# A gated Fourier and Hyena encoder layer: where ScalarE's sigmoids and operand roundings stand in the F and H projections

## The chip, the cores and the metric

The kernel runs on one core of one Trainium2 chip. The metric is the device time of one execution, in microseconds, lower is better. A core has five engines with a queue each, and a queue is worked through in order: TensorE (PE in the profile, its weight loads PEld), VectorE (DVE), ScalarE (ACT), GpSimd (POOL) and SyncE (SP). Here SP and POOL issue the transfers (DMA) of the stage in question.

## The reference, cut to what matters

Two sequences of 1024 rows of 1024 channels (`x_prompt` and `x_sample`) go through the same layer. Only its end bears on this change:

```python
def encoder_layer(x, ...):
    p = rmsnorm(x, g_pre) @ w_in
    fv, fg, hv, hg, mg = jnp.split(p, ...)
    ...                                       # fz: 2-D Fourier transform of fv; z: Hyena branch of hv
    y_f = (fz * jax.nn.silu(fg)) @ w_fourier_out
    y_h = (z * jax.nn.silu(hg)) @ w_hyena_out
    g_f, g_h = jnp.split(jax.nn.sigmoid(mg + b_merge), 2, axis=-1)
    out = (g_f * y_f + g_h * y_h) @ w_out
    return x + rmsnorm(out, g_post)
```

All arrays are float32.

## The kernel before, in words

The phases run one after the other: the Fourier transform, the Hyena branch with its filters, the gates of the second sequence (`phase_gates`), and `phase_out`, which holds the two projections `y_f` and `y_h` and then, in `last_rows`, the product with `w_out`, the norm and the residual. The gates' raw values (`mg` before bias and sigmoid) and the operands `fz * silu(fg)` and `z * silu(hg)` lie in DRAM tensors `d_g` and `d_sh` by then.

A float32 product is made of three matmuls of rounded numbers. `split` (line 168) rounds a tile on ScalarE (line 171, a CAST in the trace) to its high part and subtracts that on VectorE (line 181) to get the low part; `mm3` then multiplies high by high, high by low and low by high.

`phase_out` goes over four units: two sequences, two halves of 512 positions each. Each unit has two passes of eight tiles. The F pass (`pyf`, operands `sf`, weights `w_fo`) makes the eight 128-channel tiles of `y_f`, the H pass (`pyh`, operands `sh`, weights `w_ho`) those of `y_h`. That is 64 tiles in all. In a tile, `project` (line 1115 on) asks `weight` for two halves of the weights (128 x 512 each: a DMA on POOL's queue at line 1108, rounding on ScalarE, subtraction on VectorE), and each half feeds 12 matmuls, so a tile has 24. There are three buffers for weight halves: two in the pool `wp`, one in `op`, taken in turn by the counter `nw`.

Around the matmuls of a tile stand:

- `operand` (line 1090 on): loads one of the eight operand tiles that the *next* pass will read (DMA on SP's queue, line 1097) and rounds it at once. Operands have one buffer each for F and for H, so a load can go once the last pass that read the buffer is over.
- `gated` (line 1123): loads the gate tile `g` (line 1126, SP's queue, three buffers), takes its sigmoid in place on ScalarE (line 1127), and multiplies with the sums on VectorE.
- in the H pass, an add of the two products into `yf` and its store to `d_m` (line 1209, SP's queue).
- `beside` (line 1136): in units 1 and 2, preparation of `w_out` for the last stage, four blocks in all: a load `oraw` at tile 1 or 9 and, two tiles later, casts `bh` and `th` on ScalarE and sums and subtractions (`osum`, `bl`, `tl`) on VectorE; in unit 3 similar work for `t1` and, in `sum4`, for `t4`. Its ScalarE instructions are kept behind the tile's sigmoid, its loads behind the gate's load.

The order of instructions in each engine's queue is not simply that of the program. A planner orders all of them by program order as priority and by its own estimate of times. `tc.issue_after(x)` adds only this: the instructions in its block that run on x's engine come later in that engine's queue than x. Instructions of the block on other engines are not bound by it.

Of the kernel before, what the change touches and what calls it, by code (L numbers as in the profile page):

```python
# [9 lines left out]
F32 = mybir.dt.float32  # L10
F32R = mybir.dt.float32r
I32 = mybir.dt.int32
AF = mybir.ActivationFunctionType
# [148 lines left out]
class K:  # L162
# [626 lines left out]
    def conv_back(self, n, ct, B, ws):  # L789
# [3 lines left out]
        for g, pairs in GROUPS:  # L793
# [34 lines left out]
            def tt(name):  # L828
                return ws.tile([P, 512], F32, tag="tt", name=name, bufs=4)
# [3 lines left out]
            elif g == 3:  # L833
                S_, D_ = tt("S"), T[1]
                self.add("dve", S_, T[1], Tp)
# [243 lines left out]
    def phase_out(self):  # L1079

        tc, nc, a = self.tc, self.nc, self.a
        wp, xp = self.wp, self.xp
        units = [(b, half) for b in range(NB) for half in range(2)]
        with ExitStack() as es:
            pool = lambda n: es.enter_context(tc.tile_pool(name=n, bufs=1, reuse_waits="tile"))
            bl, sp, oc, sc, op = pool("bl"), pool("sp"), pool("oc"), pool("sc"), pool("op")
            self.nw = 0

            def operand(i, nm, k):

                b, half = units[i]
                src = (self.d_g[b][0] if nm == "f" else self.d_g[b][4] if b else self.d_sh[b])[k][:, 512 * half:512 * half + 512]
                t = xp.tile([P, 2, 512], F32R, tag=f"x{'hl'[k // 4]}{k % 4 + 4 * (nm == 'h')}", name=f"s{nm}{k}", bufs=1)
                r = t[:, 1].bitcast(F32)
                nc.sync.dma_start(r, src)
                self.split(t[:, 0], t[:, 1], r, "dve", "act")
                return t[:, 0], t[:, 1]

            def weight(w, dt, q):


                own = self.nw % 3 == 2
                self.nw += 1
                pool, nb = (op, 1) if own else (wp, 2)
                r = pool.tile([P, 512], F32, tag="w", name="wr", bufs=nb)
                nc.gpsimd.dma_start(r, a[w][dt][:, 512 * q:512 * q + 512])
                h = pool.tile([P, 4, P], F32R, tag="wh", name="wh", bufs=nb)
                l = pool.tile([P, 4, P], F32R, tag="wl", name="wl", bufs=nb)  # L1110
                self.split(h.rearrange("p a b -> p (a b)"), l.rearrange("p a b -> p (a b)"), r, "dve", "act")
                return h, l

            def project(i, nm, w, dt, S):
                ps = self.psum("mm", 4, f"py{nm}")
                for q in range(2):
                    h, l = weight(w, dt, q)
                    for kk in range(4):
                        k = 4 * q + kk
                        self.mm3(ps, (h[:, kk], l[:, kk]), S[k], k == 0, k == 7)  # L1120
                return ps

            def gated(i, dt, ps, sec, bias, out):
                b, half = units[i]
                g = wp.tile([P, 512], F32, tag="gt", name="g", bufs=3)
                self.fetched = nc.sync.dma_start(g, self.d_g[b][sec][dt][:, 512 * half:512 * half + 512])
                self.opened = nc.scalar.activation(g, g, AF.Sigmoid, bias=self.bm[:, bias:bias + 1])
                out = g if out is None else out
                self.mul("dve", out, ps, g)
                return out  # L1130

            BH, BL, TH, TL = [], [], [], []

            def beside(i, dt):

                with tc.issue_after(self.fetched.ins), tc.issue_after(self.opened.ins):
                    if i in (1, 2):
                        k, part = 2 * i - 2 + dt // 8, dt % 8  # L1140
                        if part == 1:
                            self.raw = load(k)
                        elif part == 3:
                            blocks(k, self.raw)
                    if (i, dt) == (3, 1):
                        T1.append(sum1())
                    elif (i, dt) == (3, 4):
                        h, l = T1.pop()
                        for k in range(4):
                            self.split(h[:, k], l[:, k], l[:, k].bitcast(F32), "dve", "act")  # L1150
                            T1.append((h[:, k], l[:, k]))

            def load(k):
                r = sc.tile([P, 4, 512], F32, tag="raw", name="oraw", bufs=1)
                for i in range(2):
                    nc.sync.dma_start(r[:, 2 * i:2 * i + 2].rearrange("p a b -> p (a b)"),
                                      a["w_out"][(k + 4 * i) * P:(k + 4 * i + 1) * P])
                return r

            def blocks(k, r):  # L1160
                s = sc.tile([P, 4, 512], F32, tag="sum", name="osum", bufs=1)
                h, l = [bl.tile([P, 3, 512], F32R, tag=f"{t}{k}", name=f"{t}{k}", bufs=1) for t in ("bh", "bl")]
                self.split(h[:, 0], l[:, 0], r[:, 0], "dve", "act")
                self.split(h[:, 1:3], l[:, 1:3], r[:, 2:4], "dve", "act")
                BH.append(h)
                BL.append(l)
                self.sums(s, r)
                h, l = [bl.tile([P, 2, 512], F32R, tag=f"{t}{k}", name=f"{t}{k}", bufs=1) for t in ("th", "tl")]
                self.split(h, l, s[:, 1:3], "dve", "act")
                TH.append(h)  # L1170
                TL.append(l)
                for j in range(2):
                    nc.sync.dma_start(self.d_t[j][:, k], s[:, 3 * j])

            T1, T4 = [], []

            def sum1():
                h, l = [sc.tile([P, 4, 512], F32R, tag=t, name=n, bufs=1) for t, n in (("raw", "t1h"), ("sum", "t1l"))]
                nc.sync.dma_start(l.bitcast(F32), self.d_t[0])
                return h, l  # L1180

            def sum4(k):
                h, l = [sp.tile([P, 512], F32R, tag=f"yf{2 * k + j}", name=f"t4{'hl'[j]}{k}", bufs=1) for j in range(2)]
                r = l.bitcast(F32)
                nc.sync.dma_start(r, self.d_t[1][:, k])
                self.split(h, l, r, "dve", "act")
                T4.append((h, l))

            with tc.issue_after(self.copied.ins):
                S = {(0, "f"): [operand(0, "f", k) for k in range(8)]}  # L1190
            gp = oc.tile([P, D], F32, name="gp")
            nc.sync.dma_start(gp, a["g_post"][0].partition_broadcast(P))
            for i, (b, half) in enumerate(units):
                Yf = []
                S[i, "h"] = []
                for dt in range(8):
                    ps = project(i, "f", "w_fo", dt, S[i, "f"])
                    S[i, "h"].append(operand(i, "h", dt))
                    y = sp.tile([P, 512], F32, tag=f"yf{dt}", name=f"yf{dt}", bufs=1)
                    Yf.append(gated(i, dt, ps, 5, dt, y))  # L1200
                    beside(i, dt)
                S[i + 1, "f"] = []
                for dt in range(8):
                    ps = project(i, "h", "w_ho", dt, S[i, "h"])
                    if i + 1 < len(units):
                        S[i + 1, "f"].append(operand(i + 1, "f", dt))
                    g = gated(i, dt, ps, 6, 8 + dt, None)
                    self.add("dve", Yf[dt], Yf[dt], g)
                    nc.sync.dma_start(self.d_m[i][:, :, dt], Yf[dt].rearrange("p (t c) -> p t c", t=4))
                    beside(i, 8 + dt)  # L1210
                    if i == 3 and dt % 2 == 1:
                        sum4(dt // 2)
            block = lambda j: [(BH[k][:, j], BL[k][:, j]) for k in range(4)]
            T = [[(TH[k][:, j], TL[k][:, j]) for k in range(4)] for j in range(2)]
            self.last_rows(units, block(0), block(1), block(2), T1, T[0], T[1], T4, gp, op)
# [196 lines left out]
```

## Time and profile before

| | us |
|---|---|
| median of three runs | 2494.66 |
| lowest and highest of them | 2486.66, 2496.76 |
| the profiled execution, its own time | 2485.07 |
| span in its profile, first to last instruction | 2483.2 |
| granted TensorE clock | 0.997 of full |
| first and last matmul start of the two projections | 1955.5, 2319.5 |

The profile is of one execution. A row of its timeline reads: start in us, duration in us, engine, line of the kernel, operation, out<-in by the program's names, shapes, number of merged instructions, and in brackets how long the engine stood idle before it and what ended that. Rows of groups give the total busy time, the mean of one in ns, and the idle time just before. Tile names used here: `wr` raw weights, `wh` and `wl` their high and low parts, `g` a gate, `sf` and `sh` the operands, `oraw` raw `w_out`.

### The profile page before, as it was taken

What the parts mean: (1) busy time and instruction counts of PE and PEld (TensorE: products, weight loads), DVE (VectorE), ACT (ScalarE), POOL (GpSimd) and SP (SyncE); (2) the same over time, 40 slices, a digit from 0 to 9 for tenths busy, and PEclk for the clock granted to TensorE, in tenths of its full rate; (3) what the DMA queues carried; (4) which work ended last, traced back from release to release, by engine and by line L of the source; (5) the groups of instructions that cost most, each with busy time, mean ns of one, the idle gap of its engine ahead of it and who ended that gap; (6) DMA issues with size and microseconds to landing.
All of it is one profiled execution on the core that took longest, in us unless ns stands there. A gap on an engine that the chain in (4) does not pass through costs nothing.

```text
span 2483.2 us, 37239 instructions
## 1 busy us (share of the span) xinstructions
PE 2407.4 (97%) x13184; PEld 2081.4 (84%) x13184; DVE 1955.9 (79%) x3737; ACT 1102.2 (44%) x2043; POOL 498.6 (20%) x514
## 2 busy tenths in 40 slices
PE   6999999999989999999999999999999999999998
PEld 6988888888878888888888888887888787878786
DVE  7786788888798999999889999876655456655677
ACT  5546666666653333333222233333443445444443
POOL 1331222212233333441000000212000111212121
PEclk9999999999999999999999999999999999999999
DMA  7536545444555554545343443435443567675543
GB/s 272 191 113 225 196 157 162 162 163 158 177 184 184 180 174 167 171 154 193 123 149 137 137 141 123 140 132 182 168 163 136 196 219 252 237 245 201 161 166 127
DMA packets 224867, 429.39 MB, mean 173 GB/s; under 512 B 23510, under 2 KB 87223, under 8 KB 224168
## 3 DMA queue, kind: packets, MB, share of 16 engines
q1 hardware_dynamic: 197868, 332.29, 40.1%
q0 software_dynamic: 26624, 94.70, 10.9%
q8 instruction: 104, 1.70, 0.3%
q14 instruction: 83, 0.68, 0.1%
q10 hardware_dynamic: 188, 0.02, 0.0%
HBM read 290.60 MB, written 136.31 MB: 172 GB/s over the span
## 4 chain that ended last, share of the span: by engine, by line
PE 44%; DMA 5%; DVE 3%; issue 1%; ACT 1%; SPq 0%; DVEq 0%; POOL 0%; ACTq 0%
PE pin L194 14%; PE pg L194 8%; PE po L194 6%; PE pyf L194 5%; PE pT L194 4%; PE pyh L194 4%; PE pX L194 3%; DMA oraw<-in_w_out 1%; PE tph L785 1%; DMA xraw<-d_x 1%; DMA mraw<-d_m 1%; DMA sh<-d_g 1%; DMA wr<-in_w_fo 1%; DMA wh<-d_w 0%; DMA d_m<-yf 0%
## 5 line engine op out<-in xcount | busy, mean ns | idle before, releaser
L194 PE MATMUL pin<-xh,wh 128*128 128x512 f32 x1440 | 563.8, 392 | 4.4 <-DVE v L177 1.8
L194 PE MATMUL pin<-xh,wl 128*128 128x512 f32 x1440 | 563.0, 392 | 1.6 <-POOL wl L181 1.6
L194 PE MATMUL pin<-xl,wh 128*128 128x512 f32 x1440 | 564.2, 392 | 0.0
L181 POOL TENSOR_TENSOR wl<-wr,wh 128x512 fp32r<-128x512 f32 x132 | 250.0, 1895 | 1132.2 <-ACT wh L171 1093.5
L194 PEld LDWEIGHTS pin<-xh,wh 128*128 128x128 f32 x1440 | 271.1, 188 | 54.6 <-DVE v L177 2.0
L194 PEld LDWEIGHTS pin<-xh,wl 128*128 128x128 f32 x1440 | 271.3, 188 | 51.6 <-POOL wl L181 2.5
L194 PEld LDWEIGHTS pin<-xl,wh 128*128 128x128 f32 x1440 | 271.3, 188 | 49.5
L171 ACT CAST wh<-wr 128x512 fp32r<-128x512 f32 x260 | 159.8, 618 | 227.2 <-PE pin L194 102.6
L194 PE MATMUL pT<-cinv,yh 128*128 128x256 f32 x1024 | 193.2, 283 | 0.5 <-ACT yh L171 0.5
L194 PEld LDWEIGHTS pT<-cinv,yh 128*128 128x128 f32 x1024 | 165.5, 191 | 10.1 <-ACT yh L171 0.9
L181 DVE TENSOR_TENSOR t<-pX,k 128x1024 f32<-128x1024 f32 x128 | 155.6, 1216 | 11.0 <-PE pX L194 7.6
L194 PE MATMUL pyh<-sh,wh 128*128 128x512 f32 x512 | 157.9, 391 | 3.5 <-ACT wh L171 3.5
L194 PE MATMUL pX<-bh,cfwd 128*128 128x256 f32 x768 | 160.4, 287 | 0.6 <-DVE t L181 0.6
L194 PE MATMUL pyf<-sf,wh 128*128 128x512 f32 x512 | 157.6, 391 | 1.6 <-ACT wh L171 1.6
L194 PE MATMUL pT<-cinv,yl 128*128 128x256 f32 x512 | 145.8, 285 | 5.1 <-DVE yl L181 5.0
L171 ACT CAST yh<-y 128x512 fp32r<-128x512 f32 x128 | 79.7, 622 | 158.6 <-DVE y L181 125.5
L171 ACT CAST bh<-b 128x512 fp32r<-128x512 f32 x144 | 88.9, 621 | 119.5 <-DVE b L181 81.2
L181 DVE TENSOR_TENSOR wl<-wr,wh 128x512 fp32r<-128x512 f32 x128 | 87.2, 686 | 67.1 <-ACT wh L171 67.0
L194 PEld LDWEIGHTS pX<-bh,cfwd 128*128 128x128 f32 x768 | 125.5, 190 | 4.0 <-DVE t L181 1.0
L181 DVE TENSOR_TENSOR bl<-b,bh 128x512 fp32r<-128x512 f32 x144 | 110.3, 767 | 21.9 <-ACT bh L171 21.8
L194 PEld LDWEIGHTS pyh<-sh,wh 128*128 128x128 f32 x512 | 95.5, 188 | 25.4 <-ACT wh L171 6.2
L194 PEld LDWEIGHTS pyf<-sf,wh 128*128 128x128 f32 x512 | 95.6, 188 | 23.1 <-ACT wh L171 3.7
(348 smaller groups left out, 5385.6 us busy)
## 6 DMA issues: line engine op xcount, KB each, us to landing
k<-d_k SPq DMA_DIRECT2D x128, 512.0 KB, 4.0
wr<-in_w_in SPq DMA_DIRECT2D x132, 256.0 KB, 3.1
d_g<-gt SPq DMA_DIRECT2D x124, 256.0 KB, 2.3
d_k<-kt SPq DMA_DIRECT2D x128, 128.0 KB, 2.2
d_k<-kt SPq DMA_DIRECT2D x64, 256.0 KB, 2.3
wr<-in_w_fo POOLq DMA_DIRECT2D x64, 256.0 KB, 3.6
g<-d_g SPq DMA_DIRECT2D x64, 256.0 KB, 3.9
wr<-in_w_ho POOLq DMA_DIRECT2D x64, 256.0 KB, 3.5
```

The source lines that it names most:

```text
L171: self.rounded = nc.scalar.copy(h, src)
L181: e.tensor_tensor(out, a, b, op=op)
L194: return self.nc.tensor.matmul(out, lhsT, rhs, start=start, stop=stop, skip_group_check=shared)
L785: nc.tensor.transpose(tp[:, q * P:(q + 1) * P], eo[:, e, q], self.ident)
```

## The change

Three things. First, `operand` only loads; its rounding is a function of its own, `rounded`. Second, a new function `ahead` is called once a tile: it rounds the operand that was loaded one tile earlier, with its ScalarE instruction placed behind the tile's second weight rounding (`self.weighed`), and then loads the next operand; after the pass one more call rounds the eighth. Third, the gate's sigmoid in `gated` is placed behind the same weight rounding. The first pass's eight operands are still rounded together.

```diff
                 t = xp.tile([P, 2, 512], F32R, ...)
-                r = t[:, 1].bitcast(F32)
-                nc.sync.dma_start(r, src)
-                self.split(t[:, 0], t[:, 1], r, "dve", "act")
+                nc.sync.dma_start(t[:, 1].bitcast(F32), src)
+                return t
+
+            def rounded(t):
+                self.split(t[:, 0], t[:, 1], t[:, 1].bitcast(F32), "dve", "act")
                 return t[:, 0], t[:, 1]
...
                 self.split(h..., l..., r, "dve", "act")
+                self.weighed = self.rounded
                 return h, l
...
+            def ahead(i, nm, dt):
+                S_ = S.setdefault((i, nm), [])
+                with tc.issue_after(self.weighed.ins):
+                    if dt:
+                        S_[-1] = rounded(S_[-1])
+                if dt < 8:
+                    S_.append(operand(i, nm, dt))
+
             def gated(i, dt, ps, sec, bias, out):
                 b, half = units[i]
                 g = wp.tile([P, 512], F32, tag="gt", name="g", bufs=3)
                 self.fetched = nc.sync.dma_start(g, ...)
-                self.opened = nc.scalar.activation(g, g, AF.Sigmoid, bias=...)
+                with tc.issue_after(self.weighed.ins):
+                    self.opened = nc.scalar.activation(g, g, AF.Sigmoid, bias=...)
...
-                S = {(0, "f"): [operand(0, "f", k) for k in range(8)]}
+                S = {(0, "f"): [rounded(operand(0, "f", k)) for k in range(8)]}
...
                 for dt in range(8):
                     ps = project(i, "f", "w_fo", dt, S[i, "f"])
-                    S[i, "h"].append(operand(i, "h", dt))
+                    ahead(i, "h", dt)
                     ...
+                ahead(i, "h", 8)
                 for dt in range(8):
                     ps = project(i, "h", "w_ho", dt, S[i, "h"])
                     if i + 1 < len(units):
-                        S[i + 1, "f"].append(operand(i + 1, "f", dt))
+                        ahead(i + 1, "f", dt)
                     ...
+                if i + 1 < len(units):
+                    ahead(i + 1, "f", 8)
```

More of the change, by code (lines that the diff above doesn't have):

```diff
@@ L1126, in gated @@
                 self.fetched = nc.sync.dma_start(g, self.d_g[b][sec][dt][:, 512 * half:512 * half + 512])
-                self.opened = nc.scalar.activation(g, g, AF.Sigmoid, bias=self.bm[:, bias:bias + 1])
+                with tc.issue_after(self.weighed.ins):
+                    self.opened = nc.scalar.activation(g, g, AF.Sigmoid, bias=self.bm[:, bias:bias + 1])
                 out = g if out is None else out
@@ L1194, in phase_out @@
                 Yf = []
-                S[i, "h"] = []
                 for dt in range(8):
                     ps = project(i, "f", "w_fo", dt, S[i, "f"])
-                    S[i, "h"].append(operand(i, "h", dt))
+                    ahead(i, "h", dt)
                     y = sp.tile([P, 512], F32, tag=f"yf{dt}", name=f"yf{dt}", bufs=1)
@@ L1201, in phase_out @@
                     beside(i, dt)
-                S[i + 1, "f"] = []
+                ahead(i, "h", 8)
                 for dt in range(8):
```

## The prediction

> **What bounds the kernel now.** The page comes first: TensorE (PE) is busy for 97% of the span, so time is won only where PE waits. The change touches one stage, the F and H projections, from 1955.4 to 2319.8 us.
>
> ```profile
> span 2483.2 us, 37239 instructions
> PE 2407.4 (97%) x13184; PEld 2081.4 (84%) x13184; DVE 1955.9 (79%) x3737; ACT 1102.2 (44%) x2043; POOL 498.6 (20%) x514
> ```
>
> Next, busy time by stretches: the whole stage first, then 25 us windows. The first pair after the times is PE busy and, in brackets, its matmuls; a window without a stall has 112.
>
> ```profile
> 1955.40:2319.80 364.40, 355.35 (x1539) 286.22 (x1538) 206.75 (x315) 167.91 (x270) 68.16 (x127) 1.00 0.68 227
> 1955.00:1975.00 20.00, 18.21 (x74) 13.10 (x74) 11.62 (x18) 12.70 (x20) 3.22 (x6) 1.00 0.81 294
> 1975.00:2000.00 25.00, 25.00 (x112) 20.71 (x111) 9.26 (x15) 8.68 (x14) 5.37 (x10) 1.00 0.46 149
> 2050.00:2075.00 25.00, 24.61 (x107) 19.56 (x106) 17.97 (x27) 14.29 (x24) 5.37 (x10) 1.00 0.76 258
> 2100.00:2125.00 25.00, 23.52 (x101) 18.28 (x101) 17.61 (x27) 12.60 (x20) 5.07 (x10) 1.00 0.68 213
> 2175.00:2200.00 25.00, 23.91 (x105) 19.30 (x104) 15.41 (x24) 10.91 (x19) 3.77 (x7) 1.00 0.75 261
> 2200.00:2225.00 25.00, 22.68 (x98) 17.97 (x98) 15.38 (x23) 11.45 (x18) 4.83 (x9) 1.00 0.66 209
> 2225.00:2250.00 25.00, 24.27 (x104) 18.95 (x104) 15.06 (x24) 14.46 (x25) 4.29 (x8) 1.00 0.80 277
> 2275.00:2300.00 25.00, 24.23 (x106) 19.45 (x105) 12.14 (x20) 8.76 (x14) 4.30 (x8) 1.00 0.69 221
> 2300.00:2325.00 25.00, 24.61 (x107) 19.69 (x107) 15.22 (x25) 8.90 (x15) 3.72 (x7) 1.00 0.58 183
> ```
>
> At 25/112 = 0.223 us a matmul, the missing ones cost: start (89.6 - 74) 3.5 us; near 2060 1.1; near 2110 2.5; near 2190 1.6 and 2202 3.1; near 2245 1.8; the end 1.3 + 1.1. Sum 16.0 us. All windows left out are full or lack one matmul. A second count comes from ScalarE's queue in undisturbed running:
>
> ```profile
> 2077.12 0.62 ACT L171 CAST wh<-wr 128x512 fp32r<-128x512 f32 x1 [2.05 <-PE pyf L194]
> 2078.18 0.73 ACT L1127 ACTIVATE g<-g,bm 128x512 f32<-128x512 f32 x1 [0.43 <-DMA g<-d_g]
> ...
> 2082.56 0.62 ACT L171 CAST wh<-wr 128x512 fp32r<-128x512 f32 x1 [2.05 <-PE pyf L194]
> ```
>
> Between these rows lies one more weight cast, left out; two casts make a tile: 2082.56 - 2077.12 = 5.44 us, 2.72 a half, 0.2267 a matmul. 1539 of them are 348.9 us, so 364.4 - 348.9 = 15.5 us are lost. About 16 us, 0.64% of the time, is therefore all that this stage has to give, unless the tile itself got shorter, and nothing in the change shortens it. The rows also show the order: a weight half is cast when PE has finished the half three before it (three buffers), and the sigmoid g sits between two such casts. By counting casts, the sigmoid of tile n stands behind the second cast of tile n-1 and ahead of both of tile n.
>
> Then the waits of the stage (1955 to 2322): who waited for whom, total, times, longest.
>
> ```profile
> ACT g L1127 <- DMA g<-d_g: 70.2, 49, 5.5
> ACT wh L171 <- PE pyf L194: 44.0, 32, 2.1
> ACT wh L171 <- PE pyh L194: 21.1, 15, 2.1
> ACT sh L171 <- DMA sh<-d_g: 14.0, 11, 3.9
> ACT sf L171 <- DMA sf<-d_g: 13.2, 11, 3.0
> ACT sh L171 <- DMA sh<-d_sh: 10.7, 9, 3.5
> ACT t4h L171 <- DMA t4l<-d_t: 8.2, 3, 3.7
> DVE osum L181 <- DMA oraw<-in_w_out: 3.7, 3, 1.9
> ```
>
> ScalarE stands 70.2 us at sigmoids and 14.0 + 13.2 + 10.7 = 37.9 us at operand casts, for loads. Mostly that is free, since weights run ahead. It is not free where several such waits meet the casts of an `oraw` block:
>
> ```profile
> 2107.16 0.73 ACT L1127 ACTIVATE g<-g,bm 128x512 f32<-128x512 f32 x1 [2.44 <-DMA g<-d_g]
> 2107.79 1.56 ACT L171 CAST bh<-oraw 128x512 fp32r<-128x512 f32 x2
> 2109.25 1.04 ACT L171 CAST th<-osum 128x1024 fp32r<-128x1024 f32 x1
> 2110.20 0.61 ACT L171 CAST wh<-wr 128x512 fp32r<-128x512 f32 x1
> 2110.86 0.73 PE L194 MATMUL pyh<-sh,wh 128*128 128x512 f32 x2 [0.82 <-ACT wh L171]
> 2199.09 0.73 ACT L1127 ACTIVATE g<-g,bm 128x512 f32<-128x512 f32 x1 [4.86 <-DMA g<-d_g]
> 2202.79 1.26 PE L194 MATMUL pyh<-sh,wh 128*128 128x512 f32 x4 [1.45 <-ACT wh L171]
> ```
>
> The weight cast at 2110.20 waited for nothing but its queue: a sigmoid held up by its load stood ahead of it, then 2.6 us of casts; PE started on that weight at 2110.86. The same happened at 2199 to 2202.
>
> **The change, part by part.** Durations:
>
> ```profile
> L181 DVE TENSOR_TENSOR wl<-wr,wh 128x512 fp32r<-128x512 f32 x127 | 86.5, 686 | 66.7 <-ACT wh L171 66.6
> L171 ACT CAST wh<-wr 128x512 fp32r<-128x512 f32 x127 | 77.5, 618 | 75.7 <-PE pyf L194 44.0 <-PE pyh L194 21.1 <-DMA wr<-in_w_ho 7.0
> L1127 ACT ACTIVATE g<-g,bm 128x512 f32<-128x512 f32 x64 | 46.5, 726 | 72.5 <-DMA g<-d_g 70.2 <-DVE wl L181 1.6 <-DVE g L181 0.3
> L171 ACT CAST sh<-sh 128x512 fp32r<-128x512 f32 x31 | 18.9, 623 | 24.9 <-DMA sh<-d_g 14.0 <-DMA sh<-d_sh 10.7
> ```
>
> Nothing is added or removed: the same 64 sigmoids (0.73 us), 56 operand casts (0.62) with their VectorE subtractions (0.69, as those of the weights), and all loads. Loads carry no new edge; they may leave when their buffers are free, as now. Only ScalarE's order gets lower bounds.
>
> *Sigmoids.* Tile n's moves behind the tile's own second weight cast, two casts or 5.44 us later. The longest wait of 5.5 us at the old place becomes about 0.1 if loads keep their times. Queued behind it then are an `oraw` block's casts (2.6 us) and the next tile's first weight, which becomes castable 2.72 us later and is needed 5.44 us after that; the chain behind a second weight is operand 0.62 + sigmoid 0.73 + block 2.6 = 3.95 us, so it is late by some 1.9 us at the four blocks and has 5.44 - 0.62 - 0.69 = 4.1 us in hand. The product that reads the sigmoid comes at the tile's end, 8 us after the new place: covered. Cost 0 on PE; if the loads were 5 us later still, the cover would be gone.
>
> *Operand casts.* Now all eight of a pass come when their buffers fall free, at the start of the pass before, in a bunch:
>
> ```profile
> 2053.55 1.23 DVE L181 TENSOR_TENSOR osum<-oraw 128x1024 f32<-128x1024 f32 x1 [1.91 <-DMA oraw<-in_w_out]
> 2057.82 2.49 DVE L181 TENSOR_TENSOR sh<-sh 128x512 fp32r<-128x512 f32 x4
> ```
>
> VectorE first stood for `oraw`, then did four operand subtractions in a row (2.49 us), which a weight's subtraction has to sit out. After the change one comes per tile, behind that tile's weights, so at most 0.69 us of operand work meets a weight. The wait for `oraw` stays. The last operand stands behind the pass's last weight, cast 3 halves (8.2 us) before PE reaches its next pass: covered.
>
> *The sum, against the 16.0 us.* Near 2060: 1.1 becomes 0.4 (`oraw` stays late). Near 2110: 2.5 becomes 0.3. Near 2190 and 2202: 4.7 becomes 0.8. Near 2245, a bunch of operand casts: 1.8 becomes 0.3. The end is not touched, since `t4h` gets no edge: its 2.4 us stay.
>
> ```profile
> 1962.98 1.29 ACT L171 CAST sh<-sh 128x512 fp32r<-128x512 f32 x2 [1.95 <-DMA sh<-d_sh]
> 1964.81 1.28 ACT L1127 ACT_TABLE_LOAD   x1
> 1966.10 0.72 ACT L1127 ACTIVATE g<-g,bm 128x512 f32<-128x512 f32 x1
> ```
>
> At the start the operand waits ahead of the weights go, but the first sigmoid needs only the first tile's weights ahead of it, so its load and the 1.28 us table load may now stand before the next weight; between 0 and 3.5 left, I take 2.0, nearer the rows' 1.28 + 0.72. Gains 0.7 + 2.2 + 3.9 + 1.5 + 1.5 = 9.8 us, less 0.3 for the late weight at the blocks: 9.5. The trace cannot show the new order's own waits: between -4 (every stall goes but the end's) and +5 us (0.1 a tile on 50 tiles), taken at 0.
>
> [...]
>
> The profiled execution took 2485.07 us (span 2483.2), 9.6 under the median of the three runs, 2494.66, which spread over 10 us. 2485.07 - 9.5 = 2475.6 in a like execution; from the median, **2485.2 us**.
>
> **The rivals.**
>
> *All of it goes.* With smoother VectorE the adds that free gate buffers come earlier, so loads and `t4h` too, and even the end tightens. For: bunches like the one at 2057.82 hold up VectorE's products and adds as well, on which SP's stores and the gate loads behind them wait. Against: the `oraw` and `t4h` waits have no edge in this change. Gain 15: 2479.7.
>
> *The gaps stay.* Three weight buffers, not the order, limit how far weights run ahead. For: ScalarE waited 44.0 + 21.1 us for PE to free them. Against: the casts just ahead of the stalls show no such wait (2110.20). Gain 0: 2494.7. [...]
>
> *The bunch moves to the pass's end (slower).* The order is written by a planner with its own times; the edges say only "not before". If it leaves operand casts to the end of a pass, more than three of the eight fall behind the last weights, and the next pass cannot start its tile. Price: 8 x 0.69 = 5.5 us of VectorE, less one half of PE, 2.7, so 2.8 at each of 7 pass changes: 20 us, less about 5 of gains elsewhere: 2494.66 + 15 = 2509.7. For: nothing in the edges hurries a cast. Against: the program asks for them before the next tile's weights.
>
> **How the numbers follow.** Forecast 0.56; all goes 0.20; gaps stay 0.13; bunch at the end 0.11. Half a percent (12.5 us) is about what a measurement of this kernel can tell from no change. Faster by more than that, under 2482.2: most of the second case and a tenth of the first, 0.27. Slower by more, over 2507.1: most of the last, 0.10. Between: 0.63. The range takes in the forecast with its -4 and +5 and the spread of the runs, the rival at 2479.7 and the one at 2494.7: 2475 to 2500.
>
> **What would show it.** Right: the sigmoids' wait for their loads falls from 70.2 to under 25 us; operand casts come singly, each behind a second weight cast; windows near 2110 and 2200 show 110 or more matmuls; the stage is 353 to 357 us long; its last two windows stay at 105 to 108. Wrong: weight casts that start late behind a sigmoid still waiting, stalls at pass changes with operand casts in a row, or a changed time outside the stage.

## The result, and the profile after

The change makes the kernel faster by a little: 2483.16 us, median of 22 runs (2479.62 to 2489.78), against 2490.82 us for the kernel before, median of 22 runs in the same rounds (2484.62 to 2498.11). The ratio is 0.9971, 95% interval 0.9962 to 0.9979, or 7.2 us (5.2 to 9.5).

The profiled execution after took 2484.43 us. The page looks like that of before: the same matmuls, PE as busy.

```profile
span 2482.5 us, 37206 instructions
PE 2410.8 (97%) x13184; PEld 2089.7 (84%) x13184; DVE 1955.8 (79%) x3737; ACT 1094.4 (44%) x2043; POOL 497.9 (20%) x514
```

The waits of the stage (1955 to 2322) show that the change did what its diff says. The columns are: who waited for whom, total us, times, longest.

```profile
ACT wh L171 <- PE pyf L194: 64.2, 38, 7.2
ACT wh L171 <- PE pyh L194: 57.5, 38, 2.5
ACT g L1140 <- DMA g<-d_g: 25.8, 8, 4.3
ACT t4h L171 <- DMA t4l<-d_t: 15.9, 3, 6.6
DVE osum L181 <- DMA oraw<-in_w_out: 14.6, 4, 5.4
```

ScalarE's wait at sigmoids fell from 70.2 us (49 times) to 25.8 (8 times). The waits of operand casts for their loads, 37.9 us before, are no longer among the rows of this view. In their place ScalarE waits for PE to free a weight buffer, 121.7 us where it was 65.1: more often than before, weights run as far ahead as three buffers allow. Its waits for the weights' own loads grew too, from 10.2 us to 29.6. Undisturbed, ScalarE's timeline shows the new order, with the second weight's cast, the operand and the sigmoid in a row:

```profile
2080.17 0.62 ACT L171 CAST wh<-wr 128x512 fp32r<-128x512 f32 x1 [2.10 <-PE pyf L194]
2080.70 0.61 ACT L171 CAST sh<-sh 128x512 fp32r<-128x512 f32 x1
2081.22 0.72 ACT L1140 ACTIVATE g<-g,bm 128x512 f32<-128x512 f32 x1
2082.89 0.62 ACT L171 CAST wh<-wr 128x512 fp32r<-128x512 f32 x1 [0.95 <-PE pyf L194]
2085.61 0.62 ACT L171 CAST wh<-wr 128x512 fp32r<-128x512 f32 x1 [2.10 <-PE pyf L194]
```

Casts of one kind of half are still 5.44 us apart (2085.61 - 2080.17): the tile is no shorter. What PE lost is counted by the same windows as before:

```profile
1955.00:1975.00 20.00, 16.90 (x66) 12.94 (x65) 6.77 (x11) 7.34 (x11) 3.75 (x7) 0.91 0.84 299
1975.00:2000.00 25.00, 25.00 (x112) 20.69 (x111) 12.35 (x20) 12.14 (x21) 4.83 (x9) 1.00 0.43 134
2050.00:2075.00 25.00, 24.01 (x105) 19.13 (x105) 16.07 (x24) 11.64 (x19) 4.29 (x8) 1.00 0.78 265
2100.00:2125.00 25.00, 25.00 (x112) 20.72 (x111) 19.09 (x30) 13.27 (x22) 5.00 (x10) 1.00 0.80 256
2175.00:2200.00 25.00, 24.98 (x109) 20.08 (x108) 13.66 (x21) 9.08 (x16) 4.40 (x9) 1.00 0.79 269
2200.00:2225.00 25.00, 23.41 (x104) 18.99 (x103) 17.89 (x27) 13.70 (x24) 4.83 (x9) 1.00 0.70 217
2225.00:2250.00 25.00, 25.00 (x112) 20.71 (x111) 13.25 (x21) 12.34 (x23) 4.83 (x9) 1.00 0.84 292
2275.00:2300.00 25.00, 23.07 (x98) 18.39 (x97) 13.19 (x21) 9.22 (x15) 4.83 (x9) 0.97 0.62 196
2300.00:2325.00 25.00, 24.87 (x105) 19.86 (x104) 13.25 (x22) 7.54 (x13) 2.65 (x5) 0.96 0.63 185
```

By the prediction's count (missing matmuls by 0.223 us), in us:

| place | before | predicted to be left | after |
|---|---|---|---|
| start | 3.5 | 2.0 | 5.3 |
| near 2060 | 1.1 | 0.4 | 1.6 |
| near 2110 | 2.5 | 0.3 | 0 |
| 2175 to 2225 | 4.7 | 0.8 | 2.5 |
| near 2245 | 1.8 | 0.3 | 0 |
| end | 2.4 | 2.4 | 4.7 |
| late weight at blocks | | 0.3 | in the rows above |

Two places are cured, 2175 to 2225 is halved, and near 2060, at the start and at the end it is worse. In three windows the granted clock is 0.91, 0.97 and 0.96, where before had 1.00: part of what is lost there is a slower clock, not a wait.

Profiles of one kernel differ by up to 4 us in this stage, so one of each says little about a gain of 7; there are four of before and three of after. Stage lengths, from the first `pyf` to the last `pyh` matmul start, were 364.0, 363.8, 367.5 and 365.2 us before (mean 365.1) and 362.5, 358.6 and 360.5 after (mean 360.5). That is 4.6 us from the stage. The whole profiled executions differ by 6.1 us (means 2488.7 and 2482.5), and the timed runs by 7.2 (5.2 to 9.5).

### The profile page after: what moved, and what is told of

Its sections match the earlier page's. It is cut to its first block, busy times and chain, and to the rows that moved or that the text cites. A ratio compares the mean times of both kernels' runs of the same rounds, so it can differ in the third digit from the quotient of the medians.

```text
span 2482.5 us, 37206 instructions
## 1 busy us (share of the span) xinstructions
PE 2410.8 (97%) x13184; PEld 2089.7 (84%) x13184; DVE 1955.8 (79%) x3737; ACT 1094.4 (44%) x2043; POOL 497.9 (20%) x514
## 4 chain that ended last, share of the span: by engine, by line
PE 46%; DMA 4%; DVE 2%; ACT 1%; issue 1%; SPq 0%; DVEq 0%; POOL 0%; ACTq 0%
PE pin L194 14%; PE pg L194 8%; PE pyf L194 6%; PE po L194 6%; PE pyh L194 4%; PE pT L194 4%; PE pX L194 4%; DMA xraw<-d_x 1%; PE tph L785 1%; DMA mraw<-d_m 1%; DMA t4l<-d_t 1%; DMA d_m<-yf 0%; DMA g<-d_g 0%; DMA oraw<-in_w_out 0%; DMA wh<-d_w 0%
```

## The experiments

The theories: **A**, each move removes its own stalls, so the parts add up; **B**, the operand move does the work; **C**, the sigmoid move does it and the operand move is worth little. Lost time below is the stage's length less 1535 x 0.2267 us = 348.0, in one profile each. (The stage's 64 tiles of 24 matmuls are 1536 starts, all of them in the traces, so 1535 steps.)

| kernel | median us | ratio [95%] | stage us | lost us |
|---|---|---|---|---|
| sigmoids alone | 2482.83 | 0.9969 [0.9957, 0.9981] | 356.1 | 8.1 |
| operands alone | 2486.31 | 0.9980 [0.9970, 0.9991] | 360.6 | 12.6 |
| after, operand rounded in the tile that loads it | 2485.77 | 0.9975 [0.9965, 0.9986] | 358.3 | 10.3 |
| after, operand loads spread | 2480.10 | 0.9956 [0.9939, 0.9973] | 354.9 | 6.9 |
| after, `t4` later | 2478.07 | 0.9950 [0.9934, 0.9967] | 353.7 | 5.7 |
| these two, and blocks cut in two | 2471.26 | 0.9930 [0.9913, 0.9946] | 348.2 | 0.2 |
| the same, roundings unbound | 2487.12 | 0.9990 [0.9978, 1.0001] | 363.1 | 15.1 |

Ratios are against the kernel before on the same chip; its median was 2491.43 for the first four rows, 2490.49 for the next two and 2488.87 for the last.

**Sigmoids alone** (on the kernel before).

```diff
                 self.split(h..., l..., r, "dve", "act")
+                self.weighed = self.rounded
...
-                self.opened = nc.scalar.activation(g, g, AF.Sigmoid, ...)
+                with tc.issue_after(self.weighed.ins):
+                    self.opened = nc.scalar.activation(g, g, AF.Sigmoid, ...)
```

> Only the sigmoids are put behind the tile's second weight; operands are loaded and rounded together as before. Theory A (sigmoids waiting for loads and bunches of operand roundings each hold up weights, in different places): the stalls near 2110 and 2202 us go, those near 2060, 2190 and 2245 stay; ratio to the kernel before 0.9985 (0.998 to 0.999). Rival B (the bunches alone matter): 0.9994 or more. Rival C (the sigmoids alone matter): 0.997 or less, as the whole change. In A and C ScalarE's wait of sigmoids for their loads falls from 70 to under 30 us.

Measured 0.9969, as much as the whole change: C's figure. B's is excluded by the interval; A's range, 0.998 to 0.999, only touches its upper end. The sigmoids' wait is 19.9 us (under 30 in A and C). Its waits for loads:

```profile
ACT g L1129 <- DMA g<-d_g: 19.9, 15, 2.9
ACT sf L171 <- DMA sf<-d_g: 14.0, 10, 3.3
ACT sh L171 <- DMA sh<-d_g: 13.2, 10, 3.7
ACT sh L171 <- DMA sh<-d_sh: 11.9, 11, 3.3
```

The operand casts wait 39.1 us, as before (37.9), and it costs nothing that the time shows. What hurt, then, would be these waits on top of the sigmoids' 70.2, in a queue whose weight casts have 4.1 us in hand by the prediction's estimate; that reading is argued.

**Operands alone** (on the kernel after).

```diff
-                with tc.issue_after(self.weighed.ins):
-                    self.opened = nc.scalar.activation(g, g, AF.Sigmoid, ...)
+                self.opened = nc.scalar.activation(g, g, AF.Sigmoid, ...)
```

> Only the operand roundings are moved (one tile later, behind the second weight); the sigmoids are left free. Theory A: 0.9985 (0.998 to 0.999), the stalls at pass starts go and one near 2110 or 2202 stays, the sigmoids' wait for loads stays over 50 us. Rival B: 0.997 or less. Rival C: 0.9994 or more.

Measured 0.9980, the figure of A; C's is excluded by the interval, and B's 0.997 is its lower end. In its waits the sigmoids stand as long as ever:

```profile
ACT g L1139 <- DMA g<-d_g: 77.3, 37, 5.2
```

Yet 0.20% came. With the 0.31% of sigmoids alone the parts make 0.51%, and the whole has 0.29% (0.21 to 0.38). From the three intervals the difference is 0.22%, give or take 0.18 (an estimate that takes them as independent), so the parts do not add up, though not by much more than the noise, and A falls too. Both moves thin out the same queue; that either takes away part of the same stalls is the likely reason, argued from this sum.

**The operand rounded in the tile that loads it**, still behind that tile's weight.

```diff
-                with tc.issue_after(self.weighed.ins):
-                    if dt:
-                        S_[-1] = rounded(S_[-1])
                 if dt < 8:
-                    S_.append(operand(i, nm, dt))
+                    t = operand(i, nm, dt)
+                    with tc.issue_after(self.weighed.ins):
+                        S_.append(rounded(t))
```

> As the changed kernel, but an operand is rounded in the tile that loads it, still behind that tile's second weight. If the delay by a tile matters: the first rounding of each pass stands ahead of the next tile's first weight and waits for a load that can leave only when the pass before has ended; ScalarE stands 6 to 9 us there, PE loses 1 to 3 us at each of 7 pass changes, ratio to the kernel before 0.999 to 1.005, so slower than the changed kernel. If the delay is of no account (the edge alone does it): 0.997 as the changed kernel, with operand waits for loads under 5 us.

Measured 0.9975, with an interval that overlaps the change's own: the delay by a tile is of little account here. No operand cast waits for its load in this run's view of the stage's waits. The loads are issued so early, all eight at the start of a pass, that they have landed in either case.

**Operand loads spread.** The second gate's load was late at the start of the stage. In the kernel after, its timeline reads:

```profile
1963.69 7.70 SPq L1138 DMA_DIRECT2D g<-d_g  x4
1964.50 1.28 ACT L1140 ACT_TABLE_LOAD   x1
1965.79 0.72 ACT L1140 ACTIVATE g<-g,bm 128x512 f32<-128x512 f32 x1
1969.59 0.72 ACT L1140 ACTIVATE g<-g,bm 128x512 f32<-128x512 f32 x1 [3.08 <-DMA g<-d_g]
1970.22 0.60 ACT L171 CAST wh<-wr 128x512 fp32r<-128x512 f32 x1
1970.88 1.22 PE L194 MATMUL pyf<-sf,wh 128*128 128x512 f32 x2 [3.10 <-ACT wh L171]
1971.90 0.63 PE L194 MATMUL pyf<-sf,wl 128*128 128x512 f32 x1
1972.32 1.05 PE L194 MATMUL pyf<-sf,wh 128*128 128x512 f32 x2
1973.18 0.63 PE L194 MATMUL pyf<-sf,wl 128*128 128x512 f32 x1
```

The second sigmoid stood 3.08 us for its load, the third tile's weight stood behind it, and PE idled 3.10 us. The load itself was held up on SP's queue, by a store of the gates that it reads (`d_g<-gt`), as SP's waits around the stage's start (1950 to 1972) show:

```profile
SPq L1138 <- DMA d_g<-gt: 8.0, 3, 4.2
```

Ahead of and between these stores stand the eight operand loads of the next pass, before the change and after it: both kernels issue them within 6 us around the stage's start. The experiment puts each operand load behind the previous tile's gate load:

```diff
-                    S_.append(operand(i, nm, dt))
+                    with tc.issue_after(self.fetched.ins) if self.fetched else ExitStack():
+                        S_.append(operand(i, nm, dt))
...
+            self.fetched = None
```

> As the changed kernel, with each operand load on SP's queue put behind the gate load of the tile before, so that the eight loads of a pass no longer leave in a row ahead of gate loads. If the changed kernel's largest stall (3.3 us near 1967, after which PE ran 3.4 us at half clock) comes from the second gate's load standing behind eight operand loads: that stall shrinks to under 1 us and the half clock there goes, gain 3 to 5 us on the changed kernel, ratio to the kernel before 0.9955 (0.995 to 0.9965). If that load is late for another reason (the weights' own loads, or transfers of the stage before): the stall stays over 2 us and the ratio is 0.997.

Measured 0.9956, as expected; the interval also takes in the 0.997 of the other case, so it is the profile that decides. The second gate's load now leaves 1.8 us after the stage's first matmul (1962.0) and not 7.3 after it (1956.4), and PE has no stall in the first twenty tiles:

```profile
1963.76 0.43 SPq L1139 DMA_DIRECT2D g<-d_g  x1
```

The stores that the gates' loads wait for also land sooner when the operand loads don't all leave beside them. From the DMA issues of that time (1950 to 1972; count, size, median us from issue to landing), first the kernel after, then spread loads:

```profile
d_g<-gt SPq DMA_DIRECT2D x3, 256.0 KB, 8.2
```

```profile
d_g<-gt SPq DMA_DIRECT2D x4, 256.0 KB, 2.8
```

The medians hold few stores. The 8.2 is the one of 1955.39, the only one of the three whose landing the trace tells, and SP stood 4.2 us for it ahead of the second gate's load. The 2.8 is the middle one of 2.1, 2.8 and 5.5, and the 2.1 left well ahead of the stage. The store in that place took 6.2 us in the first profile of before, 6.6 in the second of after and 7.1 in the third. So the bunch seems to cost twice: stores and gate loads take their turn among the operand loads in the queue, and the store that a gate load needs is longer under way beside them. How much each costs was not tried apart. Once issued, the second gate's load is no faster: 5.9 us to landing in the kernel after, 6.5 with the loads spread.

**`t4` later.** The end's stall is a cast that waits for its load with a weight's cast behind it, as the kernel after shows in ScalarE's timeline:

```profile
2295.99 0.62 ACT L171 CAST t4h<-t4l 128x512 fp32r<-128x512 f32 x1 [5.55 <-DMA t4l<-d_t]
2296.51 0.61 ACT L171 CAST wh<-wr 128x512 fp32r<-128x512 f32 x1
```

```diff
-                nc.sync.dma_start(r, self.d_t[1][:, k])
-                self.split(h, l, r, "dve", "act")
+                with tc.issue_after(self.fetched.ins):
+                    nc.sync.dma_start(r, self.d_t[1][:, k])
+                with tc.issue_after(self.weighed.ins):
+                    self.split(h, l, r, "dve", "act")
...
-                    if i == 3 and dt % 2 == 1:
-                        sum4(dt // 2)
+                    if i == 3 and dt in (5, 7):
+                        sum4(dt // 2 - 2)
...
+            for k in (2, 3):
+                sum4(k)
```

> As the changed kernel, but each t4 block in the last unit is loaded and rounded four tiles later than now in program order (the first behind tile 61's second weight). If the stall near 2295 (2.0 us, and 1.7 more at half clock) is ScalarE standing 5.6 us at the first t4 rounding ahead of a weight: it goes, with ScalarE's wait for t4 loads among these tiles under 1 us, gain on the changed kernel 2 to 4 us, ratio to the kernel before 0.9955 to 0.9965. If the weights are late there for their own loads: the stall stays and the ratio is 0.997.

Measured 0.9950, a little more than expected. The wait fell from 15.9 us to 2.7, where under 1 was expected, and no stall is left in the last four tiles:

```profile
ACT t4h L171 <- DMA t4l<-d_t: 2.7, 2, 1.8
```

**Three cures together.** What remained lay in the tiles behind the four `w_out` blocks. In the kernel after, first a row of ScalarE, then VectorE's, and PE's last:

```profile
2070.18 1.14 ACT L171 CAST wh<-wr 128x512 fp32r<-128x512 f32 x2
2068.56 2.02 DVE L181 TENSOR_TENSOR bl<-oraw,bh 128x512 fp32r<-128x512 f32 x2
2070.50 1.22 DVE L181 TENSOR_TENSOR tl<-osum,th 128x1024 fp32r<-128x1024 f32 x1
2071.63 1.29 DVE L181 TENSOR_TENSOR wl<-wr,wh 128x512 fp32r<-128x512 f32 x2
2072.37 0.50 PE L194 MATMUL pyf<-sf,wl 128*128 128x512 f32 x1 [0.79 <-DVE wl L181]
```

The first of these two weights is rounded by about 2070.8, and its subtraction starts only at 2071.63: VectorE has 2.02 + 1.22 us of a block's subtractions ahead of it. So, on top of the last two edits, `bh` and `bl` stay two tiles behind the load and `osum`, `th` and `tl` come two tiles after them:

```diff
                         elif part == 3:
-                            blocks(k, self.raw)
+                            self.osum = blocks(k, self.raw)
+                        elif part == 5:
+                            sums(k, self.raw, self.osum)
```

> Spread operand loads, late t4 blocks, and in each of the four w_out blocks the sums and their rounding two tiles after the first roundings (now all in one tile). In the run with spread loads alone 1.1, 1.1 and 1.6 us were left near 2071, 2159 and 2204, each behind VectorE's subtractions of a block, and 1.8 + 1.1 at t4. If these are the causes: nearly all of it goes, stage 349 to 351 us, gain 5 to 7 us on spread loads alone, ratio 0.993 to 0.994. If moving work only moves the stall: a stage of 354 us or more and 0.9955.

Measured 0.9930, as expected, 2471.26 us: the fastest of all kernels here. The stage, 348.2 us, is a little shorter than the 349 to 351 that were expected. In a window over the stage PE is busy throughout, and the clock is full:

```profile
1958.80:2307.30 348.50, 348.50 (x1538) 288.18 (x1537) 208.32 (x319) 165.69 (x272) 68.18 (x128) 1.00 0.71 239
```

The stage is at its floor (348.2 us against 348.0 for 1535 steps) with the same three buffers for weights. The cut moves `th`'s cast on ScalarE (1.05 us) away from the weights along with VectorE's part, so VectorE's share alone is not shown. Every gap went by order alone, so the measurement decides against the rival in which three buffers, not the order, set the limit.

**The same, roundings unbound**: the operand is rounded in the tile that loads it, with no edge.

```diff
-                with tc.issue_after(self.weighed.ins):
-                    if dt:
-                        S_[-1] = rounded(S_[-1])
...
-                        S_.append(operand(i, nm, dt))
+                        t = operand(i, nm, dt)
+                    S_.append(rounded(t))
```

> As the run with three cures, but operands are rounded in the tile that loads them, with no bound on where: of the change only the sigmoids' place is left, with the three cures. If the roundings' place matters once loads are spread: they wait for loads ahead of weights again at pass starts, 0.5 to 1 us lost at most of 7 pass changes, stage 352 to 355 us, ratio 0.9945 to 0.9955. If spreading the loads already spreads the roundings: no loss, stage 348 to 350 us, ratio 0.993.

Measured 0.9990: both cases that had been set down missed, and nearly all of the gain is gone. The casts now meet loads that leave later:

```profile
ACT sf L171 <- DMA sf<-d_g: 49.5, 20, 8.2
ACT sh L171 <- DMA sh<-d_sh: 26.9, 12, 5.7
ACT sh L171 <- DMA sh<-d_g: 25.8, 13, 4.3
```

That is 102.2 us of waits, with up to 8.2 us in one, ahead of weights that have some 4 in hand by the prediction's estimate. So the operand move adds little to the sigmoid move while loads leave in a bunch (0.9971 against 0.9969), and becomes needed once they are spread. Whether the edge or the delay alone would do there was not tried.

**Both kernels again**, three more profiles of before and two more of after:

> The kernel before, for a second profile. The first one, at 2485.07 us, lay 5.8 us under the median of 22 runs. If the two projections' own length varies from run to run: a stage clearly longer than 364.0 us here. If the runs differ by what lies outside the stage (short stretches at half clock in earlier stages): the stage is again 363 to 365 us.

> The changed kernel, for a second profile. In the first the stage took 362.5 us, of which two stretches at half clock (3.4 us each, after PE gaps of 3.3 and 2.0 us) cost 3.4. If these are its usual course: 362 to 363 us again, with half clock near 1970 and 2298. If they hang on small differences in landing times: 356 to 360 us and one of the two, or both, missing.

> Third profile of the kernel before. The two profiles so far have the stage at 364.0 and 363.8 us and no half clock in it, with PE gaps up to 1.7 us; in other kernels gaps of 2 us and more were followed by 3.4 us at half clock. If the kernel before now and then falls over that edge, near 2110 or 2203: 365 to 368 us and half clock there. If not: 363.5 to 364.5 us.

> Fourth profile of the kernel before, for the same question: 365 to 368 us with half clock in the stage, or 363.5 to 364.5 us without.

> Third profile of the changed kernel. The first had 362.5 us with two stretches at half clock, the second 358.6 us with none. If the gap near 1967 sits at the edge: again one of the two lengths, 358 to 359 or 360 to 363 us, according to the stretches at half clock, 1.7 us each.

The stages were 363.8, 358.6, 367.5, 365.2 and 360.5 us; each lies in one of the two ranges that had been set down for it. The last three have stretches of half clock, the first two none. Here is the one in the second repeat of the kernel before, its window and then PE's timeline:

```profile
2200.00:2225.00 25.00, 22.27 (x85) 17.54 (x84) 13.93 (x21) 9.43 (x14) 4.82 (x9) 0.86 0.66 204
```

```profile
2207.06 0.73 PE L194 MATMUL pyh<-sh,wh 128*128 128x512 f32 x2 [1.29 <-ACT wh L171]
2209.23 1.22 PE L194 MATMUL pyh<-sh,wh 128*128 128x512 f32 x2 [1.44 <-ACT wh L171]
2210.25 0.63 PE L194 MATMUL pyh<-sh,wl 128*128 128x512 f32 x1
2210.68 1.05 PE L194 MATMUL pyh<-sh,wh 128*128 128x512 f32 x2
```

From 2210.25 to 2210.68 a single matmul took 0.43 us, nearly twice the usual 0.2267.

## Why the prediction was right, and where its sum was not

**The mechanism held.** The sigmoids' wait fell to 25.8 us ("under 25" was said), operand casts come one by one behind a second weight, the window near 2110 is full, and so is the one near 2245. Two of its signs did not come: the window from 2200 has 104 matmuls, not 110 or more, and of the last two the first has 98, not 105 to 108. The budget held too: 16 us of stalls was all that this stage had to give, and the three cures gave it (ratio 0.9930, or 17.4 us; 365.1 - 348.2 = 16.9 in the profiles of the stage). The prediction's second count took 1539 matmuls, three more than the stage has; with 1535 steps it gives 16.0, as the first.

**That the number is so near is luck: two errors offset each other.** The forecast was 2485.2, the median of 22 runs is 2483.16. The base, a median of three runs, was 3.8 us above the median of 22 (2494.66 against 2490.82). The gain was set at 9.5 and came out at 7.2 in the timed runs, and at only 4.6 in the profiles of the stage, which came out at 360.5 us where 353 to 357 was said. Nor is half a percent the least that can be told from no change, as the prediction had it: the interval here is 0.09% to either side.

**The steps that failed**, as the prediction put them, with the three profiles of after. Lost time is counted here tile by tile: from a tile's first matmul start to the next tile's, less 24 x 0.2267 = 5.44 us.

- *"between 0 and 3.5 left, I take 2.0"* at the start. Left in the first four tiles were 5.3, 3.4 and 4.6 us (3.5 in the profile of before that the prediction read). Only the first sigmoid with its table load had been counted. The one that mattered was the second: it too stands ahead of the third tile's weight, and its load comes late (3.08 us at 1969.59), held by a store among a bunch of operand loads that the change leaves where it was. With that bunch spread, the stall is gone.
- *"less 0.3 for the late weight at the blocks"*. With what was said to be left near 2060, 2110 and 2190 to 2202, 1.8 us in all; units 1 and 2, which hold the four blocks, lost 4.4, 4.9 and 5.2 (8.4 in that profile of before). The chain was costed on ScalarE alone, 3.95 us against 4.1 in hand. VectorE's part, 2.02 + 1.22 us ahead of the next `wl`, was left out. Cutting the block in two, on top of the other two cures, removed these stalls.
- *"the new order's own waits ... taken at 0"*. The term was not 0, and part of it is the half clock: two stretches of 3.4 us in the first profile of after, none and one in the others, some 1.7 us each. The before's own four profiles have none, none, 6.8 and 3.4 us of it. It is not a term of the sum at all, and at the start it came behind one gap of over 3 us, where the first profile of before has three small stalls (0.5, 1.1 and 1.8).
- *The end, 2.4 us untouched*: right in kind. Left in the last eight tiles were 4.8, 2.4 and 2.7, of which about 1.7 in the first is half clock.

**The rivals.** That all gaps stay is excluded, by the interval and by the full windows. That a bunch of operand casts moves to the pass's end did not happen: they come one a tile, behind second weights, and the eighth of a pass behind a sigmoid. That everything goes did not happen with this change; with its order corrected it did.

**What stays open** is the 2.6 us between the profiles' 4.6 in the stage and the 7.2 of the timed runs. The stage's share lies below the interval's lower end of 5.2, from seven profiles that differ among themselves by up to 4 us. That the whole profiled executions differ by 1.5 us more than the stage has a reason in the traces: ahead of the stage, where both kernels have the same code, the clock records hold 10.2, 27.3, 27.3 and 30.7 us at half clock in before and 23.9, 6.8 and 30.7 in after, and half of the difference of the means is 1.7 us. In the timed runs the clock does not make the gain: its mean is 0.993 in the 22 runs of after and in the 57 of before that ran beside the experiments. So the 2.6 us may be scatter of seven profiles; that is an argument, not shown.

## What to carry to other kernels

In a queue that is worked through in order, a prefetched operation that waits for its load costs nothing, as these runs suggest (39.1 us of operand waits in the run with sigmoids alone, with no cost that the time shows), until the waits ahead of the next urgent operation add up to more than that operation has in hand; put such operations behind the urgent one, and then look again at what else stood in the same queues. Cost every engine of the chain and the queue that issues the loads, not only the engine that is edited: here the gains that were missing lay in VectorE's subtractions (2.02 + 1.22 us ahead of a weight's) and in a bunch of loads on SP's queue (3.08 us of waiting at the second sigmoid). Once the stalls had been named one by one, order alone cured them here: three small moves gave another 0.4%, without a buffer more.

## What the runs showed of the hardware

The unexpected thing is the half clock after short gaps. In the profile of after the granted clock is 0.50 in two stretches of 3.41 us, from 1970.67 and from 2298.35; in the second repeat of before there are 6.8 us of it. Matmuls are then 0.43 us apart instead of 0.2267, which costs about 1.7 us for 3.41 (an estimate: half of the stretch). A gap is taken here from one matmul's start to the next, less 0.2267; the idle time in a row's brackets is some 0.16 shorter. Such stretches followed single gaps of PE of 3.26 and 2.01 us in the first profile of after, of 2.73 in its third and of 2.61 in the run that rounds the operand in the tile that loads it, and a pair of gaps in a short time (1.45 and 1.61) in the second repeat of before. They did not follow a gap of 2.41 in the second profile of after, nor a pair of 1.62 and 1.03 in the first of before. So in these runs no length between 2.0 and 2.4 us decides alone; the gap of 2.01 us cost about 3.7 with its stretch, the one of 2.41 only itself. Why the clock falls is not shown.
